# Transposes of attention tied behind products of the projection that comes next, on one core

## The chip, the cores and the metric

The kernel runs on one core of one Trainium2 chip. The metric is device time in microseconds (us) of one execution; a lower time is better.

## What is computed

One decoder block over 512 tokens of width 1024 in float32. The input is normalised and multiplied by one wide matrix `w_in`; its columns are the queries, keys, values and gates of two attention branches, two merge gates and a forget gate. Cut to what matters here:

```
h = rms_norm(x, norm_g);  proj = h @ w_in
fq, fk, fv, fz, mq, mk, mv, mz, ga, gb, fl = split_cols(proj, ...)
y_fox  = fox_attention(norm(fq), norm(fk), fv, log_sigmoid(fl + b_f)) * silu(fz)
y_moba = moba_attention(rope(norm(mq)), rope(norm(mk)), mv)           * silu(mz)
merged = sigmoid(ga + b) * (y_fox @ w_fox) + sigmoid(gb + b) * (y_moba @ w_moba)
out    = x + merged @ w_out
```

Each branch has 8 heads of width 64. Both attentions are causal softmax attentions at this length (the second one has two blocks of 256 keys, and it selects more than there are).

## The kernel before, in words

Every float32 factor is split into a high and a low part in the type fp32r, and a product is three matmuls (high by high, high by low, low by high) that add up in one PSUM bank. So PE does nearly all the work, and ScalarE (ACT) and VectorE (DVE) copy and split.

**Attention.** It is done in four groups of four heads: `fa`, `fb` (fox) and `ma`, `mb` (moba). `attn_group` (L517) gives the pieces of one group:

- `Tr(pr)` (L526) transposes queries and keys of two heads: 4 transposes into the bank `p_qT` (L530) and 4 into `p_kT` (L532), each 128x128 in float32, with the data as weights and the identity as the moving operand. ACT and DVE then make the split queries and keys.
- `Aa(h)` (L563): per block of 128 queries the logits `lg` (L572, L573), the row minimum on DVE (L575), the exponential on ACT (L577).
- `Bb(h)` (L610): ten transposes of the exponentials (L617): 4 into `p_a`, 4 into `p_b`, 2 into `p_cc`; ACT and DVE split each bank (L623, L624); eight matmuls `pv` with the values (L627, L628); ACT and DVE join the parts.
- `Yp(pr)` (L660) multiplies by the gate and by the inverse sums.

So a group has 2x8 + 4x10 = 56 such transposes, and the four have 224. Sixteen others (L249, L501, L597, L674) are not touched.

**Fillers.** Between these pieces the kernel writes units of projection that attention doesn't depend on: for `fa` the units of fqb, fkb, fvb and mqa; for `fb` mka, mva, mza; for `ma` mqb, mkb, mvb; for `mb` mzb, wf0, wf1, wf2; then wf3 after the last group. A unit of a query, key or value (`unit`, L396, with `unit_mm`, L308) is 24 matmuls with 256 moving columns (L315 to L317) into one of the two banks `pj`, and an evacuation by ACT, for a value by ACT and DVE (L352, L353). A unit of a gate (`unit_z`, L422, with `tr_mm`) is 24 matmuls with 512 columns, and a unit wf (`unit_f`, L700, with `br_mm`) 12 with 512. `filler` (L1024) makes the list of units; each one first calls `pump` (L189), which loads and splits the weights of units up to three steps ahead.

**What sets the order.** `inter` (L1034, called at L1105) writes pieces and units in turn, in proportion to their numbers. The order in which they are written is a rank, and no more: `schedule_with_timeline_sim=True` (L1233) has a planner lay out each engine's queue in advance on its own timeline; where the instruction of the highest rank isn't ready there, it puts a later one first. The chip then runs each queue strictly in that order, waiting on semaphores only for data and buffers. `tc.issue_after` (in `behind`, L119) adds an edge that lets an instruction be queued only after a given one of the same engine; it adds no semaphore. The transposes use the three banks `tp`, the logits the two banks `lg`, the values' products the one bank `pv`.

Of the kernel before, what the change touches and what calls it, by code (L numbers as in the profile page):

```python
# [13 lines left out]
P = 128  # L14
# [15 lines left out]
def fox_moba_kernel(ctx: ExitStack, tc, xT, x, w_in, w_fl, w_fox, w_moba, w_out, cst, rope, out):  # L30
# [60 lines left out]
    def col(c, n=1):  # L91
        return cs[:, c:c + n]
# [212 lines left out]
        for i, (a, b) in enumerate(pairs):  # L305
            T.matmul(o, a, b, start=(i == 0), stop=(i == n - 1))

    def unit_mm(p, name, t, hfs=(0, 1), first=True, last=True):  # L308
        n = 264 if name == "fka" else CW
        for hf in hfs:  # L310
            hi, lo = chunks[name][hf]
            for k in range(4):
                kk = 4 * hf + k
                st = slice(t * P, (t + 1) * P)
                T.matmul(p[:, :n], Gh[:, kk, st], hi[:, k, :n], start=(kk == 0), stop=False)  # L315
                T.matmul(p[:, :n], Gh[:, kk, st], lo[:, k, :n], start=False, stop=False)
                T.matmul(p[:, :n], Gl[:, kk, st], hi[:, k, :n], start=False, stop=(kk == KT - 1))  # L317

    def evac_qk(p, name, t):
        if name not in QN:  # L320
# [75 lines left out]
    def unit(name, t):  # L396
        def go():
            p = pj(f"pj_{name}{t}")
            unit_mm(p, name, t)
            if name[1] == "v":  # L400
                evac_v(p, name, t)
            else:
                evac_qk(p, name, t)
        return go


    def tr_mm(p, name, c):
        cc = slice(c * P, (c + 1) * P)
        for hf in range(2):
            hi, lo = chunks[name][hf]  # L410
            for k in range(4):
                kk = 4 * hf + k
                gh, gl = Z[kk] if name[0] == "f" else (Gh[:, kk, :], Gl[:, kk, :])
                T.matmul(p, hi[:, k, cc], gh, start=(kk == 0), stop=False)
                T.matmul(p, hi[:, k, cc], gl, start=False, stop=False)
                T.matmul(p, lo[:, k, cc], gh, start=False, stop=(kk == KT - 1))

    ZS = {}

# [2 lines left out]
    def unit_z(name, c):  # L422
        def go():
            p = (tp if name == "fzb" else pj)(f"pz_{name}{c}")
            tr_mm(p, name, c)
            z = t2("y", 15, f"zs_{name}{c}")
            s = t2("y", 15, "sg") if name == "mzb" else t2("u", 4, "sg")
            if name[0] == "f":
                V.tensor_tensor(out=z, in0=p, in1=rbc, op=OP.mult)
                A.activation(s, z, AF.Tanh, scale=0.5)  # L430
                V.scalar_tensor_tensor(z, s, 1.0, z, op0=OP.add, op1=OP.mult)
            else:
                A.activation(s, p, AF.Tanh, scale=0.5)
                V.scalar_tensor_tensor(z, s, 1.0, p, op0=OP.add, op1=OP.mult)
            ZS[name[0], 2 * (name[2] == "b") + c] = z
        return go


    LR = con.tile([64, S], F32R, name="LR")
# [77 lines left out]
    def attn_group(br, half, gq, gk):  # L517
# [8 lines left out]
        def Tr(pr):  # L526
            def go():
                pq, pk = tp("p_qT"), tp("p_kT")
                for t in range(NT):
                    T.transpose(pq[:, t * P:(t + 1) * P], qn[:, t, pr * P:(pr + 1) * P], ident)  # L530
                for t in range(NT):
                    T.transpose(pk[:, t * P:(t + 1) * P], kn[:, t, pr * P:(pr + 1) * P], ident)  # L532
                for o in range(2):
                    h = 2 * pr + o
                    me, ot = (slice(0, HD), slice(HD, P)) if o == 0 else (slice(HD, P), slice(0, HD))
                    qs = t2("qs", 4, "QS", dt=F32R)
                    kh = t2("qs", 4, "KH", dt=F32R)
                    kl = KLt[o][pr]
                    A.activation(qs[me, :], pq[me, :], AF.Copy, scale=gq[me, :])
                    V.scalar_tensor_tensor(qs[ot, :], pq[me, :], gq[me, :], qs[me, :].bitcast(F32),  # L540
                                           op0=OP.mult, op1=OP.subtract)
                    A.activation(kh[me, :], pk[me, :], AF.Copy, scale=gk[me, :])
                    if direct:
                        A.activation(kh[ot, :], pk[me, :], AF.Copy, scale=gk[me, :])  # L544
                    else:
                        nc.scalar.dma_start(out=kh[ot, :].bitcast(F32), in_=kh[me, :].bitcast(F32))
                    V.scalar_tensor_tensor(kl[me, :], pk[me, :], gk[me, :], kh[me, :].bitcast(F32),  # L547
                                           op0=OP.mult, op1=OP.subtract)
                    q2 = qs
                    if fox:  # L550
                        q2 = Q2t[o]
                        lr = slice(HD, HD + 4) if o == 0 else slice(0, 4)
                        hh = hb + h
                        nc.sync.dma_start(out=q2[lr, :].bitcast(F32), in_=LR[hh:32:8, :].bitcast(F32))
                        nc.sync.dma_start(out=kl[lr, :].bitcast(F32), in_=LR[32 + hh:64:8, :].bitcast(F32))
                        if direct:
                            V.tensor_copy(q2[me, :], qs[me, :].bitcast(F32))
                        else:
                            nc.scalar.dma_start(out=q2[me, :].bitcast(F32), in_=qs[me, :].bitcast(F32))
                    st[h] = (qs, kh, kl, q2)  # L560
            return go
# [48 lines left out]
        def Bb(h):  # L610
            def go():
# [2 lines left out]
                pv = pst("pv", 1, "pv")  # L614

                def blk(dst, i, j):
                    T.transpose(dst, pts[i][:, j * P:(j + 1) * P], ident)  # L617

                def spl(p, n):
                    tag, w, bufs = ("pt", 512, 4) if n == 512 else ("pc", 256, 2)  # L620
# [67 lines left out]

    FS, MG = {}, {}

    def br_mm(p, name, br, c):
        hi, lo = chunks[name][0]
        cc = slice(c * P, (c + 1) * P)
        for k in range(4):
            yh, yl = Y[br, k]
            T.matmul(p, hi[:, k, cc], yh, start=(k == 0), stop=False)  # L696
            T.matmul(p, hi[:, k, cc], yl, start=False, stop=False)  # L697
            T.matmul(p, lo[:, k, cc], yh, start=False, stop=(k == 3))  # L698

    def unit_f(i, c):  # L700
        def go():
            j = 2 * i + c
            p = pj(f"pf{j}")
            br_mm(p, f"wf{i}", "f", c)
            if j == 0:
                f = sb.tile([P, 4, S], F32, name="f03", tag="v", bufs=2)
                FS[0], FS[1] = f[:, 0:2, :], f[:, 2:4, :]
            elif j in (4, 6):
                FS[j // 2] = sb.tile([P, 2, S], F32, name=f"f{j}", tag="qk", bufs=4)
            A.activation(FS[i][:, c, :], p, AF.Copy)  # L710
        return go
# [121 lines left out]
    def merge_a(i, c):  # L833
        if True:
            j = 2 * i + c
            p = pj(f"pm{j}")
            br_mm(p, f"wm{i}", "m", c)
            u = SG[i][:, c, :]
            V.tensor_tensor(out=u, in0=p, in1=u, op=OP.mult)
            V.tensor_tensor(out=u, in0=u, in1=FS[i][:, c, :], op=OP.add)  # L840
# [180 lines left out]
            return [unit_z(name, c) for c in range(2)]  # L1021
        return [unit(name, t) for t in range(4)]

    def filler(names):  # L1024
        res = []
        for nm in names:
            for n, u in enumerate(units(nm)):
                def go(i=first_prep[nm] + (n if nm[0] == "G" else 0), u=u):
                    pump(i)
                    u()  # L1030
                res.append(go)
        return res

    def inter(a, b):  # L1034
# [30 lines left out]
    for k, u in enumerate(fz):  # L1065
        u()
        if k < 3:
# [7 lines left out]
            ("f", "b", C_FQ, C_FK, ["mka", "mva", "mza"]),  # L1075
            ("m", "a", C_MQ, C_MK, ["mqb", "mkb", "mvb"]),
            ("m", "b", C_MQ, C_MK, ["mzb", "wf0", "wf1", "wf2"]))
    head, body, tail, gate = attn_group("f", "a", col(C_FQ), col(C_FK))
    head[0]()
    for n in range(4):  # L1080
        nxt = []

        def following(n=n, nxt=nxt):
            br, half, cq, ck = plan[n + 1][:4]
            if n == 1:
                moba_begin()
            nxt.extend(attn_group(br, half, col(cq), col(ck)))
            nxt[0][0]()
        fill = filler(plan[n][4])
        if n == 0:  # L1090
            for k in range(4):
                store = []

                at = 3 * k

                def with_sums(u=fill[at], k=k, store=store):
                    u()
                    with tc.issue_after(last_on(mybir.EngineType.DVE)):
                        store.append(make_sums(k))

                def with_store(u=fill[at + 1], store=store):
                    u()
                    store[0]()
                fill[at], fill[at + 1] = with_sums, with_store
        inter(body + ([following] if n < 3 else []) + tail, fill)  # L1105
        if n < 3:
            at = 2
            body, tail = nxt[1][:at] + gate + nxt[1][at:], nxt[2]
            gate = nxt[3]
    seq(["wf3"])  # L1110
    enter("gates")
    load_sums()
    fill = filler(["GA0", "GA1", "GB0"])
# [123 lines left out]
```

## Time and profile before

| | us |
|---|---|
| median of 3 runs | 425.62 (425.09 to 425.78) |
| the profiled execution, its own time | 425.94 |
| its span, first to last instruction | 424.2 |
| PE busy in it | 417.8 |
| DVE busy | 327.4 |
| ACT busy | 279.2 |

The span is what the views of the trace cover; the own time has 1.7 us more around it. PE is TensorE's matmuls and PEld its weight loads, each with a start and a duration. Matmuls are pipelined, so that a duration overlaps the next matmul: what one costs is the distance from its start to the start of the next. In the timeline, rows give the start, the duration, the engine, the line, the operation, out<-in, the shapes and a count; instructions alike that follow on each other are merged into one row.

### The profile page before, as it was taken

To read this page: it belongs to the slowest core of one execution; us is meant where nothing else is said; L and a number is where in the kernel's file an instruction comes from. 1 tells how busy PE (TensorE), PEld (TensorE's weight loads), DVE (VectorE), ACT (ScalarE), POOL (GpSimd) and SP (SyncE) were. 2 spreads that over 40 slices of the span, in tenths; PEclk is the share of its full clock that TensorE was granted. 3 is DMA by queue.
4 is the path that set the end of the run, shared out by engine and by line. 5 is a ranking of instruction groups with operands and counts; after the bars stand their busy time and mean duration, and the time that the engine had idled before them with its cause. 6 is when DMAs were issued, how large, how long until landed. Compare 5 with 4: busy or idle time off the path is not lost.

```text
span 424.2 us, 7682 instructions
## 1 busy us (share of the span) xinstructions
PE 417.8 (98%) x2913; PEld 388.6 (92%) x2913; DVE 327.4 (77%) x574; ACT 279.2 (66%) x527; POOL 103.8 (24%) x120
## 2 busy tenths in 40 slices
PE   8999999999999999999999999999999999999996
PEld 6998899999999998899998888899999989988885
DVE  3779977799967778678666679767979698689883
ACT  4976326778777878569757687656756535686450
POOL 1065630225235550015660100340000000022230
PEclk9999999999999999999999999999999999999999
DMA  7972334667253033212032310673052703697484
GB/s 233 392 281 87 112 100 111 181 206 199 74 176 114 26 102 100 80 45 99 27 100 68 106 53 27 229 250 117 24 178 62 236 2 110 208 259 118 99 140 159
DMA packets 24340, 56.10 MB, mean 132 GB/s; under 512 B 2808, under 2 KB 7600, under 8 KB 24304
## 3 DMA queue, kind: packets, MB, share of 16 engines
q1 hardware_dynamic: 13392, 38.11, 27.9%
q0 software_dynamic: 3392, 8.39, 8.7%
q10 hardware_dynamic: 7520, 9.11, 6.7%
q8 instruction: 23, 0.38, 0.4%
q14 instruction: 13, 0.11, 0.1%
HBM read 48.11 MB, written 6.32 MB: 128 GB/s over the span
## 4 chain that ended last, share of the span: by engine, by line
PE 96%; DMA 1%; SPq 0%; DVE 0%; issue 0%; ACT 0%
PE pb_GB L770 3%; PE pb_GA L770 3%; PE pb_GA L767 3%; PE pb_GB L767 3%; PE pb_GB L769 3%; PE pb_GA L769 3%; PE po L958 3%; PE po L957 3%; PE po L956 3%; PE pv L628 2%; PE lg L573 2%; PE pv L627 2%; PE lg L572 2%; PE pf L697 2%; PE pf L696 2%; PE pm L698 2%
## 5 line engine op out<-in xcount | busy, mean ns | idle before, releaser
L343 POOL TENSOR_TENSOR ff<-ss,mh 128x8 f32<-128x8 f32 x16 | 31.6, 1981 | 71.4 <-DVE ss L341 62.9
L575 DVE CUSTOM_DVE_ANT_0 p<-lg,mask 128x128 f32<-128x128 f32 (+1 forms) x64 | 30.9, 487 | 16.1 <-PE lg L573 15.6
L577 ACT ACTIVATE p<-p,negm 128x128 f32<-128x128 f32 (+1 forms) x64 | 35.7, 559 | 10.9 <-DVE negm L575 10.0
L905 POOL DMA_DIRECT2D wr_o<-in_w_out_dram x4 | 4.9, 1294 | 95.5 <-ACT wr_o L904 95.5
L143 DVE TENSOR_TENSOR wl_GA<-wr_ga,wh_GA 128x1024 fp32r<-128x1024 f32 x14 | 16.9, 1223 | 5.8 <-ACT wh_GA L141 3.9
L141 ACT ACTIVATE wh_GA<-wr_ga 128x1024 fp32r<-128x1024 f32 x14 | 14.7, 1061 | 9.9 <-PE pb_GA L769 5.1
L141 ACT ACTIVATE wh_GB<-wr_gb 128x1024 fp32r<-128x1024 f32 x14 | 14.6, 1059 | 9.5 <-PE pm L697 3.5
L918 ACT ACTIVATE wh_o<-wr_o 128x1024 fp32r<-128x1024 f32 x14 | 14.8, 1060 | 7.9 <-PE pb_GB L769 2.8
L572 PE MATMUL lg<-KH,QS 128*128 128x128 f32 (+1 forms) x64 | 20.0, 324 | 0.0
L919 DVE TENSOR_TENSOR wl_o<-wr_o,wh_o 128x1024 fp32r<-128x1024 f32 x14 | 17.0, 1222 | 3.8 <-ACT wh_o L918 3.8
L143 DVE TENSOR_TENSOR wl_GB<-wr_gb,wh_GB 128x1024 fp32r<-128x1024 f32 x14 | 16.9, 1222 | 3.5 <-ACT wh_GB L141 3.5
L653 DVE TENSOR_TENSOR ypair<-pv,ysh 64x512 f32<-64x512 f32 x16 | 11.0, 687 | 6.7 <-ACT ysh L652 6.3
L547 DVE SCALAR_TENSOR_TENSOR KL<-p_kT,cs,KH 64x512 fp32r<-64x512 f32 x16 | 12.0, 749 | 3.4 <-ACT KH L544 3.2
L652 ACT ACTIVATE ysh<-pv 64x512 f32<-64x512 f32 x16 | 9.5, 594 | 7.3 <-PE pv L628 4.2
L624 DVE TENSOR_TENSOR ptl<-p_a,pth 128x512 fp32r<-128x512 f32 x16 | 11.0, 685 | 4.2 <-ACT pth L623 4.2
L337 DVE TENSOR_REDUCE ss<-sq 128x8 f32<-128x512 f32 x16 | 10.9, 681 | 4.0 <-ACT sq L336 3.9
L767 PE MATMUL pb_GA<-Gh,wh_GA 128*128 128x256 f32 x48 | 13.6, 284 | 0.0
L769 PE MATMUL pb_GA<-Gl,wh_GA 128*128 128x256 f32 x48 | 13.5, 281 | 0.0
L770 PE MATMUL pb_GA<-Gh,wl_GA 128*128 128x256 f32 x48 | 13.5, 281 | 0.0
L770 PE MATMUL pb_GB<-Gh,wl_GB 128*128 128x256 f32 x48 | 13.5, 281 | 0.0
L769 PE MATMUL pb_GB<-Gl,wh_GB 128*128 128x256 f32 x48 | 13.4, 281 | 0.0
L767 PE MATMUL pb_GB<-Gh,wh_GB 128*128 128x256 f32 x48 | 13.3, 281 | 0.0
(461 smaller groups left out, 1801.8 us busy)
## 6 DMA issues: line engine op xcount, KB each, us to landing
wr_ga<-in_w_in_dram SPq DMA_DIRECT2D x8, 512.0 KB, 3.8
wr_gb<-in_w_in_dram SPq DMA_DIRECT2D x8, 512.0 KB, 4.6
wr_o<-in_w_out_dram SPq DMA_DIRECT2D x8, 512.0 KB, 11.4
xt<-in_xT_dram SPq DMA_DIRECT2D x8, 256.0 KB, 7.3
x<-in_x_dram SPq DMA_DIRECT2D x8, 256.0 KB, 6.0
s_dramh<-sum_sh ACTq DMA_DIRECT2D x8, 256.0 KB, 5.6
s_draml<-sum_sl ACTq DMA_DIRECT2D x8, 256.0 KB, 2.5
wr_wf<-in_w_fox_dram SPq DMA_DIRECT2D x4, 512.0 KB, 3.2
```

Of the source, the lines that this page charges most:

```text
L141: A.activation(hi[:, :, 0:n], src, AF.Copy)
L143: eng.tensor_tensor(out=lo[:, q, 0:n], in0=src[:, q], in1=hi[:, q, 0:n].bitcast(F32), op=OP.subtract)
L343: G.tensor_tensor(out=f2, in0=ss.rearrange("p t h -> p (t h)"), in1=mh, op=OP.pow)
L572: T.matmul(lg[:, :n], qs[:, qt], kh[:, :n], start=True, stop=False)
L575: V.tensor_tensor_reduce(pt, lg[:, :n], mask[:, 512 - n:512], -0.125, 3.0e38, op0=OP.add, op1=OP.min, accum_out=mkn[:, hh, i:i + 1])
L577: A.activation(pt, pt, AF.Exp, bias=mkn[:, hh, i:i + 1], scale=-1.0, accum_out=rs[:, hh, i:i + 1])
L767: T.matmul(o, hi[:, k, cc], lh, start=(n < 3 and c == 0 and k == 0), stop=False, skip_group_check=True)
L769: T.matmul(o, hi[:, k, cc], ll, start=False, stop=False, skip_group_check=True)
L770: T.matmul(o, lo[:, k, cc], lh, start=False, stop=(k == 3), skip_group_check=True)
L918: A.activation(wide(hi), wide(R[key, c]), AF.Copy)
L919: V.tensor_tensor(out=wide(lo), in0=wide(R[key, c]), in1=wide(hi).bitcast(F32), op=OP.subtract)
L956: T.matmul(o, gh, hi[:, c, r, :], start=(new and k == 0), stop=False, skip_group_check=True)
```

## The change

The matmuls of a unit become a generator that gives out one matmul at a time (`products`), and a `Unit` can be advanced by one step. All units of the four groups, and wf3, are made ahead and kept in the list `AHEAD`. Each of the 224 transposes of `Tr` and `Bb` goes through `turn`: it writes the transpose, and then one step of the first unit of `AHEAD` that isn't done. The transpose is tied by `issue_after` to the PE instruction written last, which is the product of the turn before it; the first transpose of each `Tr` and of each `Bb` is not tied (24 of the 224, so 200 are). The products themselves are not tied to anything. The step that writes a unit's last matmul also writes its evacuation. When the unit's own place in the order comes, it calls `pump` and writes what is left of it. No instruction is added or removed; the code of `unit_z`, `unit_f` and `merge_a` changes only in that it draws its matmuls from the generator.

```
+    def products(o, pairs):
+        pairs = list(pairs)
+        for i, (a, b) in enumerate(pairs):
+            if i:
+                yield
+            T.matmul(o, a, b, start=(i == 0), stop=(i == len(pairs) - 1))
...
+    AHEAD = []
+    def turn(o, i, first):
+        if first:
+            T.transpose(o, i, ident)
+        else:
+            with behind(mybir.EngineType.PE):
+                T.transpose(o, i, ident)
+        while AHEAD and AHEAD[0].done:
+            AHEAD.pop(0)
+        if AHEAD:
+            AHEAD[0].step()
+
+    class Unit:
...
+        def run(self):
+            pump(self.i)
+            while not self.done:
+                self.step()
...
                 for t in range(NT):
-                    T.transpose(pq[:, t * P:(t + 1) * P], qn[:, t, pr * P:(pr + 1) * P], ident)
+                    turn(pq[:, t * P:(t + 1) * P], qn[:, t, pr * P:(pr + 1) * P], t == 0)
                 for t in range(NT):
-                    T.transpose(pk[:, t * P:(t + 1) * P], kn[:, t, pr * P:(pr + 1) * P], ident)
+                    turn(pk[:, t * P:(t + 1) * P], kn[:, t, pr * P:(pr + 1) * P], False)
...
-                    T.transpose(dst, pts[i][:, j * P:(j + 1) * P], ident)
+                    turn(dst, pts[i][:, j * P:(j + 1) * P], j == 0 and i == 0)
...
+    fills = [filler(p[4], True) for p in plan]
+    wf3 = filler(["wf3"], True)
...
-    seq(["wf3"])
+    for u in wf3:
+        u()
```

More of the change, by code (lines that the diff above doesn't have):

```diff
@@ L306, in mm3, with unit_mm @@
             T.matmul(o, a, b, start=(i == 0), stop=(i == n - 1))
-    def unit_mm(p, name, t, hfs=(0, 1), first=True, last=True):
+    def unit_mm(name, t):
         n = 264 if name == "fka" else CW
[L310 to L317, printed above, removed]
+        st = slice(t * P, (t + 1) * P)
+        for kk in range(KT):
+            hi, lo = (w[:, kk % 4, :n] for w in chunks[name][kk // 4])
+            gh, gl = Gh[:, kk, st], Gl[:, kk, st]
+            yield from ((gh, hi), (gh, lo), (gl, hi))
+    def products(o, pairs):
[4 more added lines that the diff above has]
+            T.matmul(o, a, b, start=(i == 0), stop=(i == len(pairs) - 1))
     def evac_qk(p, name, t):
@@ L398, in go @@
             p = pj(f"pj_{name}{t}")
-            unit_mm(p, name, t)
+            yield from products(p[:, :264 if name == "fka" else CW], unit_mm(name, t))
             if name[1] == "v":
@@ L404, in unit, with tr_mm @@
         return go
-    def tr_mm(p, name, c):
+    def tr_mm(name, c):
         cc = slice(c * P, (c + 1) * P)
[L409 to L416, printed above, removed]
+        for kk in range(KT):
+            hi, lo = (w[:, kk % 4, cc] for w in chunks[name][kk // 4])
+            gh, gl = Z[kk] if name[0] == "f" else (Gh[:, kk, :], Gl[:, kk, :])
+            yield from ((hi, gh), (hi, gl), (lo, gh))
     ZS = {}
@@ L424, in go @@
             p = (tp if name == "fzb" else pj)(f"pz_{name}{c}")
-            tr_mm(p, name, c)
+            yield from products(p, tr_mm(name, c))
             z = t2("y", 15, f"zs_{name}{c}")
@@ L436, in unit_z, with __init__, step @@
         return go
+    AHEAD = []
[10 more added lines that the diff above has]
+    class Unit:
+        def __init__(self, i, go):
+            self.i, self.go, self.it, self.done = i, go, None, False
+        def step(self):
+            if self.it is None:
+                self.it = self.go()
+            if self.it is None or next(self.it, self) is self:
+                self.done = True
+        def run(self):
+            pump(self.i)
+            while not self.done:
+                self.step()
     LR = con.tile([64, S], F32R, name="LR")
@@ L689, in fox_moba_kernel, with br_mm @@
     FS, MG = {}, {}
-    def br_mm(p, name, br, c):
+    def br_mm(name, br, c):
         hi, lo = chunks[name][0]
@@ L695, in br_mm @@
             yh, yl = Y[br, k]
-            T.matmul(p, hi[:, k, cc], yh, start=(k == 0), stop=False)
-            T.matmul(p, hi[:, k, cc], yl, start=False, stop=False)
-            T.matmul(p, lo[:, k, cc], yh, start=False, stop=(k == 3))
+            yield from ((hi[:, k, cc], yh), (hi[:, k, cc], yl), (lo[:, k, cc], yh))
     def unit_f(i, c):
@@ L703, in go @@
             p = pj(f"pf{j}")
-            br_mm(p, f"wf{i}", "f", c)
+            yield from products(p, br_mm(f"wf{i}", "f", c))
             if j == 0:
@@ L836, in merge_a @@
             p = pj(f"pm{j}")
-            br_mm(p, f"wm{i}", "m", c)
+            for _ in products(p, br_mm(f"wm{i}", "m", c)):
+                pass
             u = SG[i][:, c, :]
@@ L1022, in units, with filler @@
         return [unit(name, t) for t in range(4)]
-    def filler(names):
+    def filler(names, ahead=False):
         res = []
@@ L1027, in filler @@
             for n, u in enumerate(units(nm)):
[L1028 to L1031, printed above, removed]
+                x = Unit(first_prep[nm] + (n if nm[0] == "G" else 0), u)
+                if ahead:
+                    AHEAD.append(x)
+                res.append(x.run)
         return res
@@ L1088, in following @@
             nxt[0][0]()
-        fill = filler(plan[n][4])
+        fill = fills[n]
         if n == 0:
```

## The prediction

> **What bounds the kernel now.** I read the page first, then the list of waits of PE, then one stretch of the windows view.
>
> ```profile
> span 424.2 us, 7682 instructions
> PE 417.8 (98%) x2913; PEld 388.6 (92%) x2913; DVE 327.4 (77%) x574; ACT 279.2 (66%) x527; POOL 103.8 (24%) x120
> PEclk9999999999999999999999999999999999999999
> ```
> ```profile
> PE warm_ps L107 <- DVE fg_pre L480: 1.5, 1, 1.5
> PE fqa L392 <- DVE wl_fqa L168: 0.7, 1, 0.7
> PE fqa L391 <- ACT Zh L131: 0.6, 1, 0.6
> ```
> ```profile
> 62.00:281.70 219.70, 219.70 (x1604) 207.07 (x1603) 167.44 (x351) 164.94 (x349) 64.40 (x76) 1.00 0.34 107
> ```
>
> The page says that PE is busy 98% at full clock. The second fence is the whole answer on PE's waits: three, all in the first matmuls, 2.8 us in sum. The third is the stretch in which every touched transpose lies: PE is busy 219.70 of 219.70 us. So there is no wait here that the change could take away. The time is the sum of what PE's matmuls cost, one after the other. The change can move it in two ways only: a matmul costs more or less because of its neighbours, or PE gets a wait that it doesn't have now.
>
> **What a transpose costs now, in a run and alone.** A busy share can't tell this; distances of starts can. First a run of ten, between products of 256 columns:
>
> ```profile
> 96.72 0.28 PE L317 MATMUL pj_fkb<-wh_fkb,Gl 128*128 128x256 f32 x1
> 96.84 0.60 PE L617 MATMUL p_a<-ident,p 128*128 128x128 f32 x4
> 97.27 0.60 PE L617 MATMUL p_b<-ident,p 128*128 128x128 f32 x4
> 97.71 0.38 PE L617 MATMUL p_cc<-ident,p 128*128 128x128 f32 x2
> 97.85 0.37 PE L315 MATMUL pj_fvb<-wh_fvb,Gh 128*128 128x256 f32 x1
> 98.05 0.28 PE L316 MATMUL pj_fvb<-wl_fvb,Gh 128*128 128x256 f32 x1
> ```
>
> Then one alone:
>
> ```profile
> 115.72 0.28 PE L316 MATMUL pj_mqa<-wl_mqa,Gh 128*128 128x256 f32 x1
> ...
> 116.31 0.27 PE L617 MATMUL p_b<-ident,p 128*128 128x128 f32 x1
> 116.34 0.48 PE L627 MATMUL pv<-pth,v_fva 128*128 128x512 f32 x1
> 116.66 0.39 PE L628 MATMUL pv<-ptl,v_fva 128*128 128x512 f32 x1
> 116.89 0.28 PE L315 MATMUL pj_mqa<-wh_mqa,Gh 128*128 128x256 f32 x1
> ```
>
> In the second, five products of 256 columns (one shown, four left out) take 116.31 - 115.72 = 0.59, 0.118 each, and one of 512 columns takes 116.89 - 116.66 = 0.23. The start of the first product behind a transpose (0.03 after it) is recorded too early, with a longer duration, so I always count to the product after that one. Run of ten: 98.05 - 96.72 = 1.33, less two products (0.236), is 1.094: **0.109 a transpose**. Alone: 116.89 - 116.31 = 0.58, less two of 512 columns (0.46), is **0.12**. The run's 0.109 holds one entry and one exit for ten, the lone transpose has both to itself. So parting a run isn't a gain; each cut costs at most 0.12 - 0.109 = 0.011. As the 0.12 is a difference of starts with two decimals (0.232 for the 512 columns would make it 0.116, and the cut 0.007), I take **0.008 us for each cut**.
>
> The dearest case in the trace is a product set into a run of four, and it is just the pattern that the change writes:
>
> ```profile
> 204.03 0.51 PE L617 MATMUL p_a<-ident,p 128*128 128x128 f32 x3
> 204.30 0.36 PE L627 MATMUL pv<-pth,v_mva 128*128 128x256 f32 x1
> 204.50 0.27 PE L617 MATMUL p_a<-ident,p 128*128 128x128 f32 x1
> 204.53 0.37 PE L317 MATMUL pj_mkb<-wh_mkb,Gl 128*128 128x256 f32 x1
> 204.73 0.28 PE L315 MATMUL pj_mkb<-wh_mkb,Gh 128*128 128x256 f32 x1
> ```
>
> 204.73 - 204.03 = 0.70 for four transposes and two products of 256 columns: less 0.236, 0.464, against 4 x 0.109 = 0.436. One cut cost 0.028 there, my upper end for the price; the lower end is 0, and below that only by a mechanism that I keep as a rival.
>
> **Why there is nothing to hide.** The loads of the same place:
>
> ```profile
> 204.50 0.19 PEld L317 LDWEIGHTS pj_mkb<-wh_mkb,Gl 128*128 128x128 f32 x1
> 204.61 0.19 PEld L315 LDWEIGHTS pj_mkb<-wh_mkb,Gh 128*128 128x128 f32 x1
> ```
>
> The product's load starts at 204.50, with the transpose in front of it, and the load after that 0.11 later, when the product itself has begun. PE looks one load ahead, not more. So a transpose with any product behind it lasts as long as that product's load, 0.11, which is what it costs in a run.
>
> The Trainium skill, in "TensorE: Matmul & The Clock Gate", section "Back-to-back issue gap", says otherwise: the spacing is set by load and matmul together, pipelined through a window of 64 instructions, and is about 81 ns for 128 columns. An estimate by that figure: 0.081 - 0.109 = -0.028 a transpose, -2.1 us for the 76 counted below. The trace disagrees: no run of transposes in it is nearer than 0.109.
>
> **How many cuts there will be.** A product written behind a transpose stands between it and the next only if the planner hasn't used it up before. That can be read from before: whether, when a transpose was reached, the fillers written ahead of it were done and none behind it had begun. Two sides of it in one head, `Bb(0)` of `fb`, written between the last unit of mka and the first of mva:
>
> ```profile
> 143.52 0.28 PE L317 MATMUL pj_mka<-wh_mka,Gl 128*128 128x256 f32 x1
> 143.64 0.60 PE L617 MATMUL p_a<-ident,p 128*128 128x128 f32 x4
> 143.99 0.36 PE L315 MATMUL pj_mva<-wh_mva,Gh 128*128 128x256 f32 x1
> ...
> 146.80 0.60 PE L617 MATMUL p_b<-ident,p 128*128 128x128 f32 x4
> ```
>
> `p_a` came exactly in written order: mka finished, mva not begun. With the change, three of the four are parted by mva's first products. `p_b` came 23 products of mva later, when what is offered behind its transposes has long gone: its ties are met and it stays a run. I went through the whole timeline like this, with the written order worked out from the proportions of `inter`. Of the 224, 90 were reached exactly in written order (76 of them tied), 116 after fillers written behind them (109 tied), and 18 ahead of fillers written before them (15 tied), all of these in `fa` and the first pieces of `fb`.
>
> - The 76: a cut each, 76 x 0.008 = **+0.61**. (13 of them lie among products of 512 columns.)
> - The 109: ties met already, **0**. Their ends: 0, or 109 x 0.008 = 0.87 if the planner pulls less ahead than now.
> - The 15: tied to products that weren't ready, so they can't go early any more; later they are parted like the others, 15 x 0.008 = **+0.12**. What they leave open in the queue is the next part.
> - Nothing is added or taken: 224 transposes, the same products, the same copies. `pump` stays at its place between the pieces, so loads, splits and DMA issues keep their rank; SP and POOL are passed by nothing. An evacuation is written at most ten products sooner, 10 x 0.118 = 1.2 us, and its engines have room (in the stretch above DVE 167 and ACT 165 of 220 us): 0. A transposed bank of four is finished 3 x 0.118 = 0.35 us later, one head 1.06 us, and PE has fillers for that time: 0.
>
> **What is queued behind a tied transpose.** The tie holds PE itself only where nothing else is ready for it. Where that could bite is here:
>
> ```profile
> 104.52 0.60 PE L530 MATMUL p_qT<-ident,qn_fqb 128*128 128x128 f32 x4
> ...
> 105.94 0.38 PE L532 MATMUL p_kT<-ident,qn_fkb 128*128 128x128 f32 x2
> ...
> 106.80 0.60 PE L617 MATMUL p_a<-ident,p 128*128 128x128 f32 x4
> 107.15 0.37 PE L315 MATMUL pj_fvb<-wh_fvb,Gh 128*128 128x256 f32 x1
> ```
> ```profile
> 105.00 0.41 DVE L353 TENSOR_TENSOR v_fvb<-pj_fvb,v_fvb 128x256 fp32r<-128x256 f32 x1
> ...
> 105.40 0.42 DVE L353 TENSOR_TENSOR v_fvb<-pj_fvb,v_fvb 128x256 fp32r<-128x256 f32 x1
> ```
>
> Two units of fvb were done, their banks not yet evacuated, and the planner filled PE with ten transposes of later rank. With the change eight of them wait for products of mqa, which are behind the other two units of fvb. PE then has the first transpose (0.11) and the logits and values between 104.87 and 105.94 (the rows left out, about 1.07): to 105.7. DVE frees the first bank at 105.41. So fvb can go on in time and PE doesn't wait: **0**. If the cover fails, the 15 are worth 15 x 0.109 = 1.6.
>
> **Sum.** 0.61 + 0.12 = 0.73: span 424.2 to 424.9, own time 425.94 to 426.7. The profiled execution is 0.32 over the median of the runs, so the median goes from 425.62 to **426.3**.
>
> **Rivals.**
>
> 1. *The ties make PE wait.* The planner lays the queue on its own timeline, and there the bank of fvb must have come free late: the chip's queue had the third unit at 107.15, 1.7 us after DVE's end. With eight transposes fewer to fill in, the planner either finds fvb ready or writes an order in which the chip waits. Price: the 15 uncovered (1.6) and the cuts (0.73) make 2.3 us: 427.9. It decides as soon as more than 0.1 us of PE's time is open there. Against it: DVE's row, and no wait of PE in 219.70 us now. Half of it is enough to be slower.
> 2. *The change doesn't do what it says.* The products are untied, so the planner may use them all ahead of the transposes, as it did for 116. Then nothing is parted and nothing waits: 425.6. Against it: the 90 reached in written order.
> 3. *A product hides the transpose's load.* If a lone transpose cost only its stream, 0.118 x 2 - 0.23 = 0.006 fixed, so (0.118 - 0.006) / 2 + 0.006 = 0.06, each cut would gain 0.05: 76 x 0.05 = 3.8 us, 421.8. The lone one at 116.31 and the pattern at 204.03 speak against it.
>
> **How the numbers follow.** The forecast has 0.60, rival 1 0.28, rival 2 0.07, rival 3 0.05. A measurement of this kernel tells about 0.2% (0.85 us) from no change. The forecast's own range is 425.8 to 427.4 (cuts at 0.002 to 0.023 for the 76); I put 0.20 of its 0.60 above 426.47, the rest within. Slower: 0.20 + 0.28 = 0.48. Same: 0.40 + 0.07 = 0.47. Faster: 0.05. The range runs from 425.3, a little below rival 2, to 428.4, rival 1 with cuts at 0.014; it leaves out rival 3 and dearer waits.
>
> **What would show it.** The list of PE's waits should hold its three rows and none from attention (rival 1: rows of `p_a`, `p_b`, `p_qT` or `pj`). In the timeline single transposes of `p_qT`, `p_kT` and `p_a` should alternate with products, `p_b` and `p_cc` mostly stay in runs; a pair of transpose and 256 columns should stand at 0.235 or a little more (rival 3: 0.18). The first product of GA, now at 277.42, should come 0.7 later. The forecast is wrong if runs are parted and the pair takes under 0.22, or if PE's busy time in attention falls below the stretch.

## The result, and the profile after

The changed kernel takes **425.86 us** (median of 20 runs), the kernel before 425.23 in as many runs beside it: ratio 1.0016, 95% interval 1.0010 to 1.0022, that is 0.4 to 0.9 us more; the medians are 0.63 apart. The forecast was 0.73 us more. (Its 426.3 was counted from 425.62, the median of three runs of the kernel before, which is 0.39 over the median of twenty.)

The page of the changed kernel, its waits of PE, and the stretch of attention in the windows view:

```profile
span 424.0 us, 7680 instructions
PE 417.7 (99%) x2913; PEld 387.6 (91%) x2913; DVE 330.9 (78%) x574; ACT 278.0 (66%) x527; POOL 105.3 (25%) x120
```
```profile
PE warm_ps L107 <- DVE fg_pre L511: 1.5, 1, 1.5
PE fqa L396 <- ACT Zh L131: 0.6, 1, 0.6
PE fqa L397 <- DVE wl_fqa L168: 0.5, 1, 0.5
```
```profile
62.00:281.70 219.70, 219.70 (x1599) 206.13 (x1598) 170.99 (x348) 164.10 (x350) 65.71 (x76) 1.00 0.34 107
```

Three things can mislead here. The span of this one execution is 0.2 us *shorter* than that of before, because PE lost less time in its first 12 us: the first transpose of attention starts 0.9 us earlier (65.16 instead of 66.03). The waits are those three of before, in another order. And PE is busy for all 219.70 us again. What tells the loss is the count: in the same 219.70 us PE got through 1599 matmuls instead of 1604. All five are products of 256 columns (980 instead of 985; of the other kinds there are as many as before). At 0.118 us each they are 0.6 us, give or take one product.

The order is the one that was forecast. `Bb(0)` of `fb` after the change, in PE's timeline, `p_a` and then `p_b`:

```profile
143.00 0.27 PE L445 MATMUL p_a<-ident,p 128*128 128x128 f32 x1
143.03 0.37 PE L322 MATMUL pj_mva<-wh_mva,Gh 128*128 128x256 f32 x1
143.23 0.27 PE L448 MATMUL p_a<-ident,p 128*128 128x128 f32 x1
...
143.92 0.28 PE L322 MATMUL pj_mva<-wl_mva,Gh 128*128 128x256 f32 x1
...
148.28 0.60 PE L448 MATMUL p_b<-ident,p 128*128 128x128 f32 x4
```

`p_a` alternates with mva's first products, `p_b` is still a run. Four pairs take 143.92 - 143.00 = 0.92, 0.23 a pair; a transpose in a run and a product cost 0.109 + 0.118 = 0.227. Two decimals at one place can't tell these apart, many places can: in the whole trace 63 products of 256 columns stand between two transposes, and from the start of the one transpose to the start of the other it is 0.232 on average, 0.005 over the 0.227. Around the 19 products of 512 columns that stand so it is 0.344, 0.003 over. So a cut costs **0.005 us** here or a little less, and the 83 of them about 0.4. Over the whole of PE's queue, transposes of 128 columns stood in 62 runs before and in 145 after: 83 cuts, where 91 were forecast.

One place is late, and no list of waits names it as idle time of PE. PE's timeline, then DVE's, of the changed kernel:

```profile
151.05 0.27 PE L628 MATMUL p_ri<-ident,rinv 128*8 128x128 f32 x1
151.07 0.42 PE L658 MATMUL pv<-pth,v_fvb 128*128 128x384 f32 x1
151.45 0.36 PE L322 MATMUL pj_mva<-wh_mva,Gh 128*128 128x256 f32 x1
151.65 0.28 PE L322 MATMUL pj_mva<-wl_mva,Gh 128*128 128x256 f32 x1
```
```profile
150.29 0.68 DVE L342 TENSOR_REDUCE ss<-sq 128x8 f32<-128x512 f32 x1
150.89 0.41 DVE L358 TENSOR_TENSOR v_mva<-pj_mva,v_mva 128x256 fp32r<-128x256 f32 x1
```

From 151.05 to 151.65 a transpose (0.11), a matmul of 384 columns (0.176) and one of 256 (0.118) should take 0.40; they take 0.60. The third unit of mva begins here, in the bank of the first, and DVE empties that bank until 151.30. The same place before:

```profile
150.96 0.41 DVE L353 TENSOR_TENSOR v_mva<-pj_mva,v_mva 128x256 fp32r<-128x256 f32 x1
```
```profile
152.41 0.28 PE L315 MATMUL pj_mva<-wh_mva,Gh 128*128 128x256 f32 x1
```

DVE was done at 151.37 and PE came at 152.41: a margin of 1.0 us. Now DVE is done at 151.30 and PE comes at 151.45, and the margin is gone: 0.2 us of waiting that PE's busy share hides, since the durations of matmuls overlap. To see which of the two moved, count from the first transpose of attention, at 66.03 before and 65.16 now. DVE's end goes from 85.34 to 86.14, 0.8 us later. PE's product goes from 86.38 to 86.29, and without the wait it would be at 86.09, 0.3 sooner. So most of the margin went on the side of DVE. One row shows what came in between there, the low part of the split keys, before and then in the changed kernel:

```profile
146.46 0.76 DVE L547 SCALAR_TENSOR_TENSOR KL<-p_kT,cs,KH 64x512 fp32r<-64x512 f32 x1
```
```profile
148.90 0.76 DVE L578 SCALAR_TENSOR_TENSOR KL<-p_kT,cs,KH 64x512 fp32r<-64x512 f32 x1
```

By the same count it comes 3.3 us later. It follows ACT's high part of the keys, and in ACT's queue the copy of the last unit of mka and a split of weights now stand ahead of that. This is read off the queues; no run changes it alone.

### The profile page after: what moved, and what is told of

It is laid out like the page before. It is cut to its first block, busy times and chain, and to the rows that moved or that the text cites. A ratio compares the mean times of both kernels' runs of the same rounds, so it can differ in the third digit from the quotient of the medians.

```text
span 424.0 us, 7680 instructions
## 1 busy us (share of the span) xinstructions
PE 417.7 (99%) x2913; PEld 387.6 (91%) x2913; DVE 330.9 (78%) x574; ACT 278.0 (66%) x527; POOL 105.3 (25%) x120
## 4 chain that ended last, share of the span: by engine, by line
PE 97%; DMA 1%; SPq 0%; DVE 0%; issue 0%; ACT 0%
PE pf L322 5%; PE pm L322 5%; PE pb_GB L799 3%; PE pb_GA L799 3%; PE pb_GA L796 3%; PE pb_GB L796 3%; PE pb_GA L798 3%; PE pb_GB L798 3%; PE po L988 3%; PE po L987 3%; PE po L986 3%; PE pj_mva L322 3%; PE pj_fva L322 3%; PE pj_fkb L322 3%; PE pj_mka L322 3%; PE pj_mqa L322 3%
## 5 line engine op out<-in xcount | busy, mean ns | idle before, releaser
L143 DVE TENSOR_TENSOR wl_GA<-wr_ga,wh_GA 128x1024 fp32r<-128x1024 f32 x14 | 17.9, 1295 | 4.3 <-ACT wh_GA L141 3.5
```

Source lines behind the costliest of these rows:

```text
L143: eng.tensor_tensor(out=lo[:, q, 0:n], in0=src[:, q], in1=hi[:, q, 0:n].bitcast(F32), op=OP.subtract)
```

## The experiments

The theories. **1: the cuts alone make the loss**, so a cut costs 0.63 / 83 = 0.0076 us, as forecast. **2: a cut costs 0.003 to 0.004, and waits that the new order makes, through the ties, are the rest.** The rival of both is that a product hides the transpose's load.

**Offers without ties** (`e1_offer_untied`). All 224 transposes are written untied:

```
-        if first:
-            T.transpose(o, i, ident)
-        else:
-            with behind(mybir.EngineType.PE):
-                T.transpose(o, i, ident)
+        T.transpose(o, i, ident)
```

> The changed kernel with its products offered as before, but no transpose tied. In the queue of PE the 240 transposes with the full identity stand in 118 runs (62 in the kernel before, 145 in the changed one), so 56 cuts instead of 83. Theory 1, cuts alone make the loss (0.63 us / 83 = 0.0076 us each): 56 x 0.0076 = 0.43 us over before, ratio 1.0010. Theory 2, a cut costs 0.004 us (0.31 us over 83 in the trace of the changed kernel) and the ties make the other 0.3 us as waits of PE: 0.2 us over before, ratio 1.0005, and no row of a matmul in attention that starts late. Rival, an offered product hides the load of the transpose: faster than before.

Measured: 425.96, ratio 1.0020 (1.0011 to 1.0028); the changed kernel beside it 425.96. So neither theory had it right: without a single tie the loss is the same. 56 of the 83 cuts come from the rank alone, as a product written between two transposes ranks between them. The late start behind `p_ri` of `fb` is there as well (0.58 us instead of 0.40, from 150.85 to 151.43), so it isn't made by ties either. That fewer cuts cost as much is no contradiction: the planner's order is another one here, and distances of starts show two more late places, 0.11 us at the logits at 73.92 and 0.15 at a value product at 253.65. With 56 x 0.005 = 0.28 and the 0.2 behind `p_ri` they make about 0.7 of the 0.78 between the medians. What these two more wait for stays open.

**Everything parted** (`e2_all_parted`). The product is tied behind its transpose too, which undoes "left untied":

```
         if AHEAD:
-            AHEAD[0].step()
+            with behind(mybir.EngineType.PE):
+                AHEAD[0].step()
```

> The changed kernel with each offered product tied behind its transpose as well, so that nearly all transposes are parted: 234 runs, 172 cuts. Theory 1 (0.0076 us a cut): 1.3 us over before, ratio 1.003, with PE's busy time in attention unbroken. Theory 2 (0.004 us a cut and waits through ties): 0.7 us from cuts and at least the 0.3 us of the changed kernel from waits, more likely 0.5 to 2, since every tie now holds: ratio 1.0025 to 1.006, with waits of 0.1 us and more visible between starts. Rival, hidden loads: faster than the changed kernel.

Measured: 435.20, ratio 1.0233 (1.0220 to 1.0247), far over both. Its windows view for the stretch of attention, its waits, and one of the places in PE's timeline:

```profile
62.00:281.70 219.70, 214.46 (x1543) 197.96 (x1542) 165.02 (x342) 159.30 (x342) 63.57 (x72) 1.00 0.32 103
```
```profile
PE p_b L448 <- DVE QS L572: 1.8, 2, 1.5
...
PE pv L659 <- ACT pth L655: 1.3, 3, 0.6
...
PE pj_fvb L322 <- DVE v_fvb L358: 0.6, 1, 0.6
```
```profile
145.50 0.39 PE L605 MATMUL lg<-KL,Q 128*128 128x128 f32 x2
147.34 0.30 PE L448 MATMUL p_b<-ident,p 128*128 128x128 f32 x1 [1.46 <-DVE QS L572]
```

Here PE really stands still: `p_b` waits 1.5 us for its bank, and the products of mva, which filled that time before and in the changed kernel, are tied behind it. The sum isn't a price of cuts: of the 10.0 us over the kernel before, PE's idle time in the stretch is 219.70 - 214.46 = 5.2, and 172 cuts at 0.005 would be 0.9. The rest is late starts that the busy share hides. The run shows what the fillers are worth when they may go first.

**The changed kernel once more** (`e3_changed_again`, no edit).

> The changed kernel once more, with a new profile. Both theories: ratio 1.0010 to 1.0022. Theory 1: the late start of 0.26 us of the values' product at 151.07 is chance and is not seen again. Theory 2: it and the 0.07 us at 104.4 are seen again, at the same instructions.

Measured: 425.96, ratio 1.0018 (1.0009 to 1.0026). The late start is there again, at the same instructions:

```profile
151.77 0.27 PE L628 MATMUL p_ri<-ident,rinv 128*8 128x128 f32 x1
...
152.35 0.28 PE L322 MATMUL pj_mva<-wl_mva,Gh 128*128 128x256 f32 x1
```

0.58 instead of 0.40. At 104.4 neither trace has anything late: from `p_qT` at 103.73 to 105.00 us (104.48 to 105.76 here) PE takes 1.27 and 1.28 us for matmuls that cost 1.28. So theory 1 is out as a whole: part of the loss is a wait that was there in both profiles.

**The price of a cut by itself** (`e5_extra_in_runs`, `e6_extra_parted`). On the kernel before, 672 transposes of a constant into the free bank, first 24 in a run behind each product of the merge gates, then one behind each matmul:

```
+    def extra(m):
+        if not EX:
+            EX.append(pst("pv", 1, "pv_x"))
+        for _ in range(m):
+            T.transpose(EX[0][:, 0:P], ones, ident)
...
                     T.matmul(o, lo[:, k, cc], lh, ...)
+            extra(24)            # e5; in e6 extra(1) behind each of the three matmuls instead
```

> The kernel before with 672 extra transposes of a constant into the free bank pv, 24 written in a run behind each of the 28 merge-gate products (24 matmuls of 256 columns each); their result isn't used. No transposes of attention change place: 91 runs instead of 62. At 0.109 each they add 73.2 us: about 498.4 us. It is the base for the run with the same transposes parted.

> The same 672 extra transposes, one written behind each matmul of the merge-gate products: 570 runs, 479 cuts more than with the runs of 24. They and the products around them wait for nothing new. Theory 1 (a cut costs 0.0076 us): 3.6 us over the one in runs. Theory 2 (0.003 to 0.004 us): 1.4 to 1.9 us over it. Rival, a product hides the load: 479 x 0.05 = 24 us less than in runs.

Measured: 500.45 in runs (2 us over the estimate; for 1.7 of them the first one waits for the bank `pv`) and 503.25 parted. Not all of the 2.8 between them is cuts: in the output stage of the parted one PE has rows of waits of 0.4 and 0.2 us that the other hasn't. A stretch with merge-gate products and extra transposes, without these waits, in the windows view, in runs and then parted:

```profile
300.00:440.00 140.00, 140.00 (x1182) 137.71 (x1180) 67.04 (x67) 46.92 (x64) 0.00 (x0) 1.00 0.21 66
```
```profile
300.00:440.00 140.00, 140.00 (x1172) 137.70 (x1170) 64.63 (x64) 43.94 (x61) 0.00 (x0) 1.00 0.20 62
```

By kinds, these are twelve transposes fewer and two products of 256 columns more: 12 x 0.109 - 2 x 0.118 = 1.1 us less done. The transposes stand in 25 runs there in the first and in 443 in the second: 1.1 / 418 = **0.003 us a cut**. Distances of starts agree: 499 products stand between two transposes in the second, 0.230 from one transpose to the next, against 0.227. The 0.0076 of theory 1 and the hidden load, which would have gained over 20 us, are refuted. In the changed kernel itself the same count gave 0.005. These transposes are of a constant and go to one bank, those are of data and go to three; which of it makes the difference, no run shows.

**The late bank** (`e7_bank_by_act`). In the changed kernel the low part of mva's values is left out (zeros), so that DVE has no part in emptying these banks:

```
+            if name == "mva":
+                G.memset(VT[name].bitcast(F32), 0.0)
...
-        V.tensor_tensor(out=v[:, t, :, HD:P], in0=pv, ...)
+        if name != "mva":
+            V.tensor_tensor(out=v[:, t, :, HD:P], in0=pv, ...)
```

> The changed kernel, where the low part of the values of mva is left out (zeros set once on GpSimd), so that ACT alone empties the banks of these four units. 141 runs. If the late start behind p_ri at 151 us is PE waiting for the bank that DVE empties late, it is gone, and the time is 0.2 to 0.3 us under the changed kernel: 425.7, ratio to before 1.0012. If DVE's evacuation isn't its cause, it stays, and the time is that of the changed kernel, ratio 1.0018. The planner writes a new order, so another place may move by as much.

Measured: 425.82, ratio 1.0015 (1.0006 to 1.0023). By time it can't be told from the changed kernel. By the timeline the late start is gone. The third unit of mva, and ACT's copy that empties its bank:

```profile
151.01 0.33 PE L607 MATMUL lg<-KL,Q 128*128 128x384 f32 x1
151.18 0.28 PE L322 MATMUL pj_mva<-wh_mva,Gh 128*128 128x256 f32 x1
151.30 0.28 PE L322 MATMUL pj_mva<-wl_mva,Gh 128*128 128x256 f32 x1
```
```profile
149.74 0.37 ACT L359 ACTIVATE v_mva<-pj_mva 128x256 fp32r<-128x256 f32 x1
```

The distances are 0.17 and 0.12, as they should be, and the bank was free at 150.11, 1.1 us ahead. The order is another one here too (the unit begins ahead of `p_ri`), so this run alone doesn't settle it. But in the three traces that have the wait, the unit's first product starts 0.15 us behind DVE's end each time: 151.30 and 151.45 in the changed kernel, 152.01 and 152.16 in its repetition, 151.09 and 151.24 without ties. DVE's evacuation is the cause of that wait; what it is worth in time stays at the 0.2 us that the timeline shows.

**A transpose where it is cheaper** (`e4_behind_128`, then `e8_behind_128_two_groups` and `e9_behind_128_one_group`). The traces show matmuls of 128 columns that take about 0.11 with a product behind them, and less with a transpose behind them. So on the kernel before, the two transposes of `p_cc` go behind the two value products of 128 columns, in all groups, in fa and ma, in fa alone:

```
-                for i in range(2, 4):
-                    blk(pc[:, (i - 2) * P:(i - 1) * P], i, 2)
-                hc = spl(pc, 256)
                 pvm(0, ha, 0, 512, True, False)
                 pvm(1, hbb, 0, 384, False, False)
-                pvm(3, hbb, 384, 128, False, False)
+                for q in range(2):
+                    with behind(mybir.EngineType.PE):
+                        T.matmul(pv[:, 384:512], vt[:, 3, h, :], hbb[q][:, 384:512], start=False, stop=False)
+                    with behind(mybir.EngineType.PE):
+                        blk(pc[:, q * P:(q + 1) * P], q + 2, 2)
+                hc = spl(pc, 256)
                 pvm(2, hc, 0, 256, False, True)
```

> The kernel before, where in each head the two transposes of p_cc are moved behind the two value products of 128 columns, one behind each, by ties. The trace of before shows such products at 0.109 with a product behind them and 0.06 to 0.09 with a transpose behind them. 32 transposes then stand behind a matmul of 128 columns (3 in before), 68 runs. If a transpose's load is shorter than a product's, each gains 0.02 to 0.045 us: 29 x 0.03 = 0.9 us less than before, ratio 0.998. If it isn't, or if the value bank held longer makes PE wait, ratio 1.000 to 1.003.

> The kernel before with the transposes of p_cc behind the two value products of 128 columns in the groups fa and ma alone (where the run with all four groups showed no new waits). 16 transposes stand behind such a matmul (3 in before), 77 runs (62). In the run with all four, the stretch from 80 to 140 us, with eight of them, was 0.33 us under before: 0.04 each. Theory (a product of 128 columns is held by the load of the next product, and a transpose's load is shorter): 13 x 0.04 less 15 cuts x 0.003 = 0.5 us less than before, ratio 0.9989. If PE waits for the splits, as in fb and mb: ratio 1.001 or more.

> The same in the group fa alone: 9 transposes behind a matmul of 128 columns, 68 runs: 6 x 0.04 less 6 x 0.003 = 0.2 us less than before, ratio 0.9995, which this measurement can hardly tell from 1; its profile should show PE's starts without a wait up to 280 us.

Measured: 441.76, ratio 1.0390 (1.0366 to 1.0414); 429.19, ratio 1.0088 (1.0073 to 1.0103); 426.54, ratio 1.0027 (1.0017 to 1.0037). All three are slower, and the idea holds all the same where nothing waits. The stretch from 80 to 140 us in the windows view, before and then with fa alone:

```profile
80.00:140.00 60.00, 60.00 (x490) 59.11 (x490) 50.87 (x112) 47.64 (x107) 22.16 (x23) 1.00 0.47 143
```
```profile
80.00:140.00 60.00, 60.00 (x493) 59.15 (x492) 46.93 (x107) 44.31 (x103) 16.71 (x16) 1.00 0.46 143
```

By kinds, four transposes and one product of 512 columns more and two products of 256 fewer in the same time: 0.4 us, give or take one matmul. At 137.79 us with fa alone, two such products, two transposes and a product of 256 columns take 0.49; less 2 x 0.109 and 0.118, that is 0.08 for each of the two. Whether a shorter load of the transpose is the reason, no run shows. But then the values come later, and behind them the banks; two of PE's waits with fa alone, and the two largest with all groups:

```profile
PE pv L628 <- DVE ptl L624: 0.3, 1, 0.3
...
PE pj_mva L315 <- DVE v_mva L353: 0.2, 1, 0.2
```
```profile
PE pv L627 <- DVE ypair L655: 5.2, 2, 3.2
PE pv L628 <- DVE ptl L624: 4.0, 4, 2.0
```

It is mva's bank again that is late in the mildest of the three. The list has only 0.5 us of waits in attention there; by distances of starts, PE takes 2.34 us from 150.80 to 153.14 for matmuls that cost 1.09, so 1.25 of the 1.4 us that this version loses lie at this one place. No version here beats the kernel before.

## Why the prediction was right, and where its sum was not

- *PE's matmuls are the time, and nothing in the change can gain.* Held: full in the stretch before and after, and fewer matmuls done in it.
- *How many cuts.* 91 forecast, 83 found, and where they were forecast: `p_qT`, `p_kT`, `p_a` parted, `p_b` and `p_cc` nearly always in runs, the main exception being the head that was a run of ten. But the ties have little to do with it; the rank makes 56 of the 83.
- *The price of a cut.* **This term was mis-sized**: 0.008 forecast, 0.005 in the changed kernel, 0.003 with the extra transposes. It came from a difference of starts with two decimals at one lone transpose. The 0.73 should have been about 83 x 0.005 = 0.4.
- *Waits: 0.* **This term was wrong too**, and made up for most of the first. The place that was examined did hold: in `fb`'s first transposes PE goes on with logits and values, and fvb resumes without a wait, as the timeline of the changed kernel has it:

```profile
105.35 0.28 PE L659 MATMUL pv<-ptl,v_fva 128*128 128x256 f32 x1
105.47 0.28 PE L322 MATMUL pj_fvb<-wh_fvb,Gh 128*128 128x256 f32 x1
```

  The wait of 0.2 us came at mva, 46 us later, where products that come a little sooner reach a bank that DVE empties 0.8 us later than before. The step that failed is the one that put the evacuations written sooner at 0 because their engines have room: DVE and ACT had room on the whole, but the order of their queues changed. It is rival 1's mechanism (a bank not yet evacuated) at another place and at an eighth of its price; the ties that it named aren't its cause.
- *The sum.* About 0.4 from cuts and 0.2 from that wait are 0.6 of the 0.63 between the medians. That the forecast of 0.73 came so near is luck in part: a price too high stood against a wait put at nothing. Why a cut costs 0.005 here and 0.003 with the extra transposes stays open.
- *The signs to look for.* The alternation came as said, and the pair at 0.232, a little under the 0.235. PE's list of waits holds its three rows as said, but that was no proof: it shows nothing of the late start. The sign at GA failed: its first product came at 275.70, sooner than before, because the planner put it ahead of the last values' products (14 of them behind it, 8 before).

## What to carry to other kernels

In a kernel whose PE is full, measure what a matmul costs next to each kind of neighbour, from distances of starts over many of them, before parting or joining runs; a price from one place with two decimals was 0.008 where the mean of many is 0.003 to 0.005. Where an order is planned in advance, a change of rank moves the margins between a producer and the bank it needs, on the side of the engines that empty the bank too: look for small margins all along the stretch, not only at the place of the edit (the one that was lost here was 1.0 us). And compare moments of two traces from a common event, not from the start. Don't tie the fillers to the work that they cover: here that cost 9 us against the changed kernel.

## What the runs showed of the hardware that was not expected

**Transposes keep the clock up.** The Trainium skill, in "TensorE: Matmul & The Clock Gate", section "Part 4: PE-mode transpose", says that the full clock doesn't engage for transposes, as they don't count as busy in the same way. In `e5_extra_in_runs` 34 of them follow on each other, and then products. PE's timeline, and the windows of the two parts:

```profile
299.53 3.87 PE L726 MATMUL pv_x<-ident,ones 128*128 128x128 f32 x34
303.16 0.36 PE L775 MATMUL pb_GA<-S2h,wh_GA 128*128 128x256 f32 x1
303.36 0.28 PE L777 MATMUL pb_GA<-S2l,wh_GA 128*128 128x256 f32 x1
```
```profile
299.80:303.10 3.30, 3.30 (x33) 3.30 (x31) 2.32 (x2) 1.40 (x2) 0.00 (x0) 1.00 0.06 22
303.20:306.00 2.80, 2.80 (x26) 2.80 (x25) 1.25 (x2) 0.00 (x0) 0.00 (x0) 1.00 0.00 0
```

The granted clock is 1.00 in both. Counted to the second product, 303.36 - 299.53 = 3.83 less 0.118 is 3.71 for 34 transposes, 0.109 each. For 3.7 us at least the trace doesn't bear out that sentence. The clock was full ahead of them, so it shows that float32 transposes keep it, not that they would raise it.

**Long waits cost twice.** In the run with all groups moved (`e4_behind_128`) PE waits 3.2 and 2.0 us around 284 to 294 us. Afterwards, in its windows view:

```profile
298.00:302.00 4.00, 4.00 (x24) 4.00 (x23) 0.69 (x1) 0.82 (x2) 1.09 (x2) 0.60 0.66 250
302.00:306.00 4.00, 4.00 (x36) 4.00 (x36) 1.05 (x1) 2.31 (x3) 0.00 (x0) 1.00 0.00 0
```

PE is busy in both, but gets through 24 matmuls in the first 4 us and 36 in the next, at granted clocks of 0.60 and 1.00; all but one are products of 256 columns. With each of the two waits the clock fell to a half, and it was back to full in between:

```profile
287.60:290.90 3.30, 2.85 (x11) 2.66 (x12) 1.78 (x3) 0.86 (x2) 0.00 (x0) 0.50 0.84 326
291.10:294.30 3.20, 1.21 (x10) 0.97 (x9) 2.29 (x4) 1.68 (x3) 0.54 (x1) 1.00 0.40 124
294.50:301.10 6.60, 6.13 (x27) 5.57 (x26) 1.12 (x2) 1.57 (x3) 2.78 (x4) 0.50 0.54 183
```

The Trainium skill, in "TensorE: Matmul & The Clock Gate", section "Why this matters for your kernels", advises against gaps of more than about 3 us, as PE then falls back to half its clock; this trace agrees for the wait of 3.2 us, and here the wait of 2.0 us was followed by half the clock too.
